# Hybrid attention, state-space and rwkv blocks on one core: decay-row loads issued from GpSimd's queue

## The chip, the cores and the metric

One core of a Trainium2 chip runs the whole program. The metric is the device time of one execution in microseconds (us), as the median of a few runs. The engines are named as in the profile: PE is the matrix engine (PEld its weight loads), DVE the vector engine, ACT the scalar engine, POOL is GpSimd, SP is the engine that here does nothing but issue DMAs. A trailing q (SPq, POOLq) marks an engine's sequencer. Each engine works through its own instructions strictly in order.

## The reference, cut to what matters

The program is a chain of blocks on 512 tokens of width 1024 (attention, a state-space scan, feed-forward layers, an rwkv scan, a second scan with matrix memory). The change lies in the state-space scan of the first block. Its decay matrix is built per chunk of 128 tokens and per head from the cumulated log decay `la`:

```python
SSD_CHUNK = 128
def step(state, inp):                       # one chunk; 4 chunks, 32 heads in 4 groups of 8
    x_, dt_, b_, c_ = inp
    la = jnp.cumsum(dt_ * a, axis=1)
    seg = la[:, :, None] - la[:, None, :]
    decay = jnp.exp(jnp.where(causal, seg, -jnp.inf))
    cb = jnp.einsum('bign,bjgn->bijg', c_, b_)
    xdt = x_ * dt_[..., None]
    y_intra = jnp.einsum('bijg,bijgh,bjghp->bighp', cb, decay, xdt)
    y_inter = jnp.einsum('bign,bghpn->bighp', c_, state) * jnp.exp(la)[..., None]
    to_end = jnp.exp(la[:, -1:] - la)
    new_state = (state * jnp.exp(la[:, -1])[..., None, None]
                 + jnp.einsum('bjgn,bjgh,bjghp->bghpn', b_, to_end, xdt))
    return new_state, y_intra + y_inter
```

## The kernel before, in words

All matmuls that matter are done in three passes of split weights: `wload` (L294 to L305) brings a 512 KB block of weights into `wraw` from SP's queue, ACT rounds it to `whi` (L302), DVE computes the rest `wlo` (L303), and PE multiplies `wlo`, `whi` and `whi` again (L311 to L313, or L394 to L396). `wraw`, `whi` and `wlo` have three buffers each, so a weight load waits for the readers of the block three before it.

In the state-space stage four groups of heads are worked through one behind another, and three strands are merged in turn: `group(g)` (the scan of group g, `ssd_core`, then its output product `ssd_out`), `ssd_in(g + 1)` (input products, convolution and transposes of the next group) and pieces of `ada_units`, a product that belongs to a later block and only fills PE's time: it loads two blocks of `ada_w` into `wraw` (L1039), multiplies them straight from there (L1042, into `pso`) and adds the result to `adr` on DVE (L1045, L1047). The fourth group's scan is merged with the gate products (`w_gate`, L849 to L851) and the rest of the `ada` pieces, and has no input products beside it.

Inside `ssd_core`, each of the 4 chunks takes 8 heads in two halves. For a half, L778 loads 4 rows of 128 cumulated log decays from `lad`, a small DRAM tensor, to all 128 partitions (tile `La`, 128 x 4 x 128, 256 KB written, rows of 512 bytes). DVE subtracts the column value and clips at zero, one head at a time (L781, four instructions), ACT takes the exponential in place (L782), DVE multiplies by the masked product of C and B (`cbm`) into `MT` (L784). PE then multiplies `MT` with `xdt` (L789). The state is carried by L804 (PE), L809 and L810 (DVE), and enters the next chunk by L796 (PE). There are 4 x 4 x 2 = 32 such loads. `La` has three buffers, so a load waits until L784 has read the half three before.

The convolution is `conv_silu` (L703 to L714): ACT evicts the product to `cacc` (L709), DVE adds three shifted terms (L711), ACT takes tanh (L713), DVE closes it into `xst`, `BT` or `CT` (L714).

The order of instructions on each engine is not that of the source: a scheduler simulates the program and sets each engine's order from when it thinks operands are there. Where a DMA is issued is therefore part of what sets the order on the other engines. At run time every engine follows the fixed order and waits on semaphores.

In this stage GpSimd has nothing to do: its last work before it are small DMAs of the attention's last step (L613, L629, L633), the next one is an addition in the last output product (L944).

Of the kernel before, what the change touches and what calls it, by code (L numbers as in the profile page):

```python
# [18 lines left out]
P = 128  # L19
# [240 lines left out]
class Kern:  # L260
# [494 lines left out]
    def ssd_core(self, pool, g, inp):  # L755

        nc, D = self.nc, self.D
# [8 lines left out]
        for c in range(4):  # L766
            ct = slice(c * P, (c + 1) * P)
            ps = self.btile()[:, :P]
            nc.tensor.matmul(ps, BT[:, ct], CT[:, ct], start=True, stop=True)
            cbm = pool.tile([P, P], F32, name="cbm")  # L770
            V_.tensor_tensor(cbm, ps, self.triu, op=ALU.mult)
            xdt = pool.tile([P, 512], F32, name="xdt")
            V_.tensor_tensor(hv(xdt), hv(xs[:, c]), bc(self.dtt[:, c, h8]), op=ALU.mult)
            MTs = []
            for half in range(2):
                E = pool.tile([P, 4, P], F32, name="La", bufs=3)
                hs = slice(8 * g + 4 * half, 8 * g + 4 * half + 4)
                nc.sync.dma_start(E, self.lad[hs, ct].unsqueeze(0).to_broadcast([P, 4, P]))  # L778
                for k in range(4):
                    h = 8 * g + 4 * half + k  # L780
                    V_.tensor_scalar(E[:, k], E[:, k], self.lat[:, c, h:h + 1], 0.0, op0=ALU.subtract, op1=ALU.min)  # L781
                S_.activation(E, E, AF.Exp)  # L782
                MT = pool.tile([P, 4, P], F32, name="MT", bufs=3)
                V_.tensor_tensor(MT, E, cbm.unsqueeze(1).to_broadcast([P, 4, P]), op=ALU.mult)  # L784
                MTs.append(MT)
                yield
            yi = self.psO.tile([P, 512], F32, name="pso")
            for k in range(8):
                nc.tensor.matmul(yi[:, k * 64:(k + 1) * 64], MTs[k // 4][:, k % 4], xdt[:, k * 64:(k + 1) * 64],  # L789
                                 start=True, stop=True)  # L790
            y = pool.tile([P, 512], F32, name="tmp", bufs=4)
            V_.tensor_tensor(hv(y), hv(xs[:, c]), bc(self.dsk[:, h8]), op=ALU.mult)
            V_.tensor_tensor(y, yi, y, op=ALU.add)
            if c > 0:
                yx = self.btile()
                nc.tensor.matmul(yx, CT[:, ct], state, start=True, stop=True)  # L796
                t = pool.tile([P, 512], F32, name="tmp", bufs=4)
                V_.tensor_tensor(hv(t), hv(yx), bc(self.ela[:, c, h8]), op=ALU.mult)
                V_.tensor_tensor(y, y, t, op=ALU.add)
            if c < 3:  # L800
                xw = pool.tile([P, 512], F32, name="tmp", bufs=4)
                V_.tensor_tensor(hv(xw), hv(xs[:, c]), bc(self.wend[:, c, h8]), op=ALU.mult)
                ps = self.btile()
                nc.tensor.matmul(ps, Bt[:, c], xw, start=True, stop=True)  # L804
                new = pool.tile([P, 512], F32, name="state")
                if state is None:
                    S_.copy(new, ps)
                else:
                    V_.tensor_tensor(hv(new), hv(state), bc(self.etot[:, c, h8]), op=ALU.mult)  # L809
                    V_.tensor_tensor(new, ps, new, op=ALU.add)  # L810
                state = new
                yield
            V_.scalar_tensor_tensor(yg[:, c], y, 0.5, zs[:, c], op0=ALU.mult, op1=ALU.mult)
            S_.activation(y, yg[:, c], AF.Square, accum_out=ss[:, c:c + 1])
# [1519 lines left out]
```

## Time and profile before

| | us |
|---|---|
| median of 3 runs | 3330.66 (3327.07 to 3337.02) |
| the profiled execution | 3335.31 |
| its span, first to last instruction | 3333.5 |
| PE busy in the span | 3125.6 (94%) |
| DVE, ACT, POOL busy | 1977.9, 1392.0, 225.0 |

The state-space scan runs from about 390 us to 830 us of the span. In a timeline a row gives start, duration, engine, line, operation, output and inputs, shape and count; in square brackets stands how long the engine was idle just before, and whose end released it. An x2 or x16 behind a row means that so many instructions of one kind ran behind one another. A wait is put down to the one event that came last.

### The profile page before, as it was taken

The numbers are of one execution on the slowest core, as the hardware profiler recorded it, in microseconds if no ns is written. First come the engines' busy times: TensorE is split into PE (matmuls) and PEld (weight loads), VectorE is DVE, ScalarE is ACT, GpSimd is POOL, SyncE is SP. The second block draws the span as 40 slices with busy tenths as digits, with TensorE's granted clock in tenths as the row PEclk, the third lists the DMA queues.
The fourth block names the chain that finished last, engine by engine and source line by source line (L and its number), as shares of the span: only waits on it lengthen the run. The fifth ranks groups of instructions, "written<-read, shape, count | busy, mean of one in ns | idle before, by whom it ended". The sixth has DMA issues, their size and how long they took to land.

```text
span 3333.5 us, 57556 instructions
## 1 busy us (share of the span) xinstructions
PE 3125.6 (94%) x23870; PEld 2490.3 (75%) x23870; DVE 1977.9 (59%) x3286; ACT 1392.0 (42%) x2387; POOL 225.0 (7%) x325
## 2 busy tenths in 40 slices
PE   8999999999999999899798999989999899999998
PEld 7777777776777788666477788678788667778887
DVE  4344576775655533557665566567385754775756
ACT  3344334333354432435444455355432454543323
POOL 0000000000100000022111111000000210000001
PEclk9999999999999999899799999989999999999999
DMA  6222344345534432434555554622222425222233
GB/s 203 87 65 71 123 151 148 117 133 193 166 119 128 129 112 95 149 102 148 164 171 185 178 181 141 238 93 94 102 95 95 139 86 188 82 104 97 95 99 108
DMA packets 216518, 431.00 MB, mean 129 GB/s; under 512 B 75114, under 2 KB 114218, under 8 KB 216000
## 3 DMA queue, kind: packets, MB, share of 16 engines
q1 hardware_dynamic: 192896, 367.59, 34.2%
q10 hardware_dynamic: 20912, 51.64, 4.2%
q0 software_dynamic: 2448, 8.09, 0.8%
q8 instruction: 187, 3.06, 0.4%
q14 instruction: 75, 0.61, 0.1%
HBM read 380.46 MB, written 46.79 MB: 128 GB/s over the span
## 4 chain that ended last, share of the span: by engine, by line
PE 75%; DVE 10%; DMA 7%; ACT 4%; issue 3%; POOL 1%; SPq 0%; ACTq 0%; POOLq 0%; DVEq 0%
PE psa L311 12%; PE psa L313 12%; PE psa L312 12%; PE psa L394 6%; PE psa L395 6%; PE psa L396 6%; PE pso L311 3%; DVE wlo L303 2%; PE pso L312 2%; PE pso L313 2%; ACT whi L302 1%; PE pso L1042 1%; DMA wraw<-in_f_up_dram 1%; PE psa L1601 1%; PE pso L789 1%
## 5 line engine op out<-in xcount | busy, mean ns | idle before, releaser
L303 DVE TENSOR_TENSOR wlo<-wraw,whi 128x1024 fp32r<-128x1024 f32 x480 | 593.5, 1238 | 497.8 <-ACT whi L302 494.9
L302 ACT CAST whi<-wraw 128x1024 fp32r<-128x1024 f32 x482 | 503.6, 1047 | 757.2 <-PE psa L396 255.9
L311 PE MATMUL psa<-xh,wlo 128*128 128x512 f32 (+1 forms) x1760 | 696.0, 397 | 12.9 <-DVE wlo L303 8.9
L313 PE MATMUL psa<-xh,whi 128*128 128x512 f32 (+1 forms) x1760 | 687.2, 391 | 0.0
L312 PE MATMUL psa<-xl,whi 128*128 128x512 f32 (+1 forms) x1760 | 685.1, 390 | 0.0
L311 PEld LDWEIGHTS psa<-xh,wlo 128*128 128x128 f32 x1760 | 338.6, 193 | 89.2 <-DVE wlo L303 11.0
L313 PEld LDWEIGHTS psa<-xh,whi 128*128 128x128 f32 x1760 | 338.2, 192 | 73.5 <-issue 5.1
L312 PEld LDWEIGHTS psa<-xl,whi 128*128 128x128 f32 x1760 | 338.9, 193 | 70.4 <-issue 2.9
L1163 DVE SCALAR_TENSOR_TENSOR fc<-psa,f_cv,fc 128x441 f32<-128x441 f32 (+2 forms) x352 | 243.4, 692 | 40.8 <-ACT fc L1152 33.9
L311 PE MATMUL pso<-xh,wlo 128*128 128x256 f32 (+1 forms) x720 | 230.7, 320 | 3.0 <-DVE wlo L303 2.1
L312 PE MATMUL pso<-xl,whi 128*128 128x256 f32 (+1 forms) x720 | 221.0, 307 | 1.0 <-DVE xl L357 1.0
L313 PE MATMUL pso<-xh,whi 128*128 128x256 f32 (+1 forms) x720 | 220.7, 307 | 0.0
L395 PE MATMUL psa<-wlo,ah 128*128 128x512 f32 x528 | 211.6, 401 | 2.7 <-DVE wlo L303 2.4
L394 PE MATMUL psa<-whi,al 128*128 128x512 f32 x528 | 209.7, 400 | 3.4 <-ACT whi L302 3.4
L396 PE MATMUL psa<-whi,ah 128*128 128x512 f32 x528 | 210.4, 399 | 0.0
L311 PEld LDWEIGHTS pso<-xh,wlo 128*128 128x128 f32 x720 | 135.9, 189 | 16.6 <-issue 6.5
L312 PEld LDWEIGHTS pso<-xl,whi 128*128 128x128 f32 x720 | 136.1, 189 | 8.7 <-DVE xl L357 1.6
L313 PEld LDWEIGHTS pso<-xh,whi 128*128 128x128 f32 x720 | 135.9, 189 | 7.9 <-issue 1.2
L395 PEld LDWEIGHTS psa<-wlo,ah 128*128 128x128 f32 x528 | 99.4, 188 | 30.0 <-DVE wlo L303 6.2
L394 PEld LDWEIGHTS psa<-whi,al 128*128 128x128 f32 x528 | 99.3, 188 | 29.6 <-ACT whi L302 4.7
L394 PE MATMUL psa<-whi,xl 128*128 128x512 f32 x288 | 116.4, 406 | 2.9 <-DVE acc L940 1.5
L396 PEld LDWEIGHTS psa<-whi,ah 128*128 128x128 f32 x528 | 99.5, 188 | 23.5
(570 smaller groups left out, 4985.1 us busy)
## 6 DMA issues: line engine op xcount, KB each, us to landing
wraw<-in_f_up_dram SPq DMA_DIRECT2D x132, 512.0 KB
wraw<-in_ada_w_dram SPq DMA_DIRECT2D x96, 512.0 KB
wraw<-in_f_dn_dram SPq DMA_DIRECT2D x66, 512.0 KB
wraw<-in_w_fi_dram SPq DMA_DIRECT2D x44, 512.0 KB
wraw<-in_ab_f_dram SPq DMA_DIRECT2D x38, 512.0 KB
wraw<-in_w_qk_dram SPq DMA_DIRECT2D x24, 512.0 KB
wraw<-in_w_xbc_dram SPq DMA_DIRECT2D x24, 512.0 KB
wraw<-in_c_f_dram SPq DMA_DIRECT2D x24, 512.0 KB
```

The source lines that it names most:

```text
L302: nc.scalar.copy(hi, raw)
L303: (eng or nc.vector).tensor_tensor(lo, raw, hi.bitcast(F32), op=ALU.subtract)
L311: mm(ps, wl, xh, start=start, stop=False)
L312: mm(ps, wh, xl, start=False, stop=False)
L313: mm(ps, wh, xh, start=False, stop=stop)
L394: mm(ps, sl, wh[:, c], start=first and k == 0, stop=False)
L395: mm(ps, sh, wl[:, c], start=False, stop=False)
L396: mm(ps, sh, wh[:, c], start=False, stop=last and k == kbn - 1)
L789: nc.tensor.matmul(yi[:, k * 64:(k + 1) * 64], MTs[k // 4][:, k % 4], xdt[:, k * 64:(k + 1) * 64], start=True, stop=True)
L1042: nc.tensor.matmul(ps[o:o + 32], self.cs[:, 4 * h + j, 22 - 2 * i:54 - 2 * i], raw[:, j * 256:(j + 1) * 256], start=h == 0, stop=h == 1, t ...
L1163: V_.scalar_tensor_tensor(o, pv[:, r0 + dr:r1 + dr, c0 + dc:c1 + dc], cw(i), o, op0=ALU.mult, op1=ALU.add)
L1601: mm(ps[h, d, b], lt[h, d, b], rt[h, d, b], start=True, stop=True, tile_position=(32 * q, 32 * q))
```

## The change

The 32 loads of L778 are issued from GpSimd's queue instead of SP's. Nothing else is written differently.

```diff
             for half in range(2):
                 E = pool.tile([P, 4, P], F32, name="La", bufs=3)
                 hs = slice(8 * g + 4 * half, 8 * g + 4 * half + 4)
-                nc.sync.dma_start(E, self.lad[hs, ct].unsqueeze(0).to_broadcast([P, 4, P]))
+                nc.gpsimd.dma_start(E, self.lad[hs, ct].unsqueeze(0).to_broadcast([P, 4, P]))
                 for k in range(4):
                     h = 8 * g + 4 * half + k
```

On SP's queue the loads leave, and the weight loads keep their order among themselves. On GpSimd's queue all 32 stand one behind another with nothing between them. The scheduler, which now sees the loads on a free queue, also sets DVE, ACT and PE in another order at some places of the stage. Numbers behind a name tell the buffers of one tile apart.

DVE at the start of the stage (`La_3155` is the first of all loads, `cacc_2832` a convolution of the first group's inputs):

```order
 L685 COPY dtla_2849<-psb_2840 128x256
 L714 SCALAR_TENSOR_TENSOR CT_2668<-ctan_2779,cacc_2774 128x512
+L781 TENSOR_SCALAR La_3155<-La_3155,dtla_2849 128x128
 L711 SCALAR_TENSOR_TENSOR cacc_2832<-psa_2800,conv1_2657,cacc_2832 128x511
 L781 TENSOR_SCALAR La_3155<-La_3155,dtla_2849 128x128
```

The first subtraction of the first load moves ahead of a convolution step that stood before it.

DVE in the first group, around the load of chunk 2, second half (`La_3582`; groups two and three have the same piece):

```order
 L784 TENSOR_TENSOR MT_3433<-La_3426,cbm_3359 128x512
 L714 SCALAR_TENSOR_TENSOR xst2_3332<-ctan_3338,cacc_3333 128x512
+L781 TENSOR_SCALAR La_3582<-La_3582,dtla_2849 128x128 x2
 L711 SCALAR_TENSOR_TENSOR cacc_3404<-psa_3372,conv1_2657,cacc_3404 128x511
 L1047 TENSOR_TENSOR adr_2645<-pso_3412,adr_2645 128x256
```

Two of its four subtractions move ahead of a convolution step and of the addition to `adr`.

DVE in the fourth group, around the load of chunk 2, second half (`La_6047`); `state_5966` is the state that L796 reads next, `wlo_5901` a block of gate weights:

```order
 L1047 TENSOR_TENSOR adr_2645<-pso_5875,adr_2645 128x256
+L781 TENSOR_SCALAR La_6047<-La_6047,dtla_2849 128x128
 L810 TENSOR_TENSOR state_5966<-psb_5964,state_5966 128x512
 L771 TENSOR_TENSOR cbm_6020<-psb_6018,masks_89 128x128
-L809 TENSOR_TENSOR state_6124<-state_5966,ela_2893 128x512
+L781 TENSOR_SCALAR La_6047<-La_6047,dtla_2849 128x128
 L303 TENSOR_TENSOR wlo_5901<-wraw_5899,whi_5900 128x1024
 L784 TENSOR_TENSOR MT_6031<-La_6024,cbm_6020 128x512
+L781 TENSOR_SCALAR La_6047<-La_6047,dtla_2849 128x128 x2
 L798 TENSOR_TENSOR tmp_6117<-psb_6115,ela_2893 128x512
-L781 TENSOR_SCALAR La_6047<-La_6047,dtla_2849 128x128 x4
```

The first subtraction of this load now stands ahead of the step that completes the state, L810; in the order before all four stood far behind it.

## Rows read from the trace of the kernel before

**Rows 1.** Stretches: length, busy of PE, PEld, DVE, ACT, POOL, clock, DMA, GB/s.

```profile
750.00:800.00 50.00, 44.25 (x263) 29.73 (x263) 29.24 (x63) 11.63 (x19) 0.00 (x0) 0.97 0.66 224
sum 440.00, PE 424.15 PEld 325.02 DVE 308.85 ACT 170.99 POOL 0.00; mean PE 47.13 PEld 36.11 DVE 34.32 ACT 19.00 POOL 0.00
```

**Rows 2.** Waits, PE, 387 to 826 us: total us, times, longest.

```profile
PE pso L1042 <- DMA wraw<-in_ada_w_dram: 6.6, 4, 3.0
PE pso L1042 <- DVE cacc L711: 5.0, 2, 2.6
PE psb L743 <- DVE xst L714: 1.2, 1, 1.2
PE psb L796 <- DVE state L810: 1.1, 2, 0.6
```

**Rows 3.** Waits, SP's queue, 360 to 830 us.

```profile
SPq L301 <- DVE wlo L303: 152.9, 34, 18.9
SPq L1039 <- PE pso L1042: 78.0, 19, 8.6
SPq L778 <- DVE MT L784: 30.6, 22, 4.2
```

**Rows 4.** Tile La: instructions (ns min/median/max), and who waits for its load.

```profile
L778 SPq DMA_DIRECT2D La<-lad x32: 377/377/750, 392.9 to 774.7; - x32
...
  DMA La<-lad: 15.3, 5
```

**Rows 5.** Timeline of all engines, 461 to 469 us, group one.

```profile
461.15 1.28 DVE L784 TENSOR_TENSOR MT<-La,cbm 128x512 f32<-128x512 f32 x2
461.86 0.98 SPq L778 DMA_DIRECT2D La<-lad  x2
465.30 0.82 SPq L1039 DMA_DIRECT2D wraw<-in_ada_w_dram  x2
465.52 0.75 DVE L711 SCALAR_TENSOR_TENSOR cacc<-psa,conv,cacc 128x511 f32<-128x511 f32 x1 [2.48 <-ACT cacc L709]
467.17 1.21 DVE L303 TENSOR_TENSOR wlo<-wraw,whi 128x1024 fp32r<-128x1024 f32 x1
468.71 0.59 PE L1042 MATMUL pso<-wraw,cs 128*32 128x256 f32 x2 [1.99 <-DMA wraw<-in_ada_w_dram]
```

**Rows 6.** DMAs that GpSimd issues: tiles B (512 KB, 512-byte rows), Wb, R; landings.

```profile
L468 POOL DMA_DIRECT2D B<-scr x2: 889/892/894, 39.6 to 50.1; - x2
DMA to landing us min/median/max: 4.4/6.4/9.8
L633 POOL DMA_DIRECT2D Wb<-dw x8: 597/611/620, 197.1 to 338.3; - x8
DMA to landing us min/median/max: 3.6/4.7/6.1
L613 POOL DMA_DIRECT2D R<-dstat x4: 564/585/774, 186.3 to 324.6; - x4
```

**Rows 7.** Timeline, SP and DVE, 388 to 442 us.

```profile
392.89 1.49 SPq L778 DMA_DIRECT2D La<-lad  x3
397.84 0.29 DVE L781 TENSOR_SCALAR La<-La,dtla 128x128 f32<-128x128 f32 x1 [1.66 <-DMA La<-lad]
438.04 0.98 SPq L778 DMA_DIRECT2D La<-lad  x2
441.80 1.66 DVE L781 TENSOR_SCALAR La<-La,dtla 128x128 f32<-128x128 f32 x8 [3.19 <-DMA La<-lad]
```

**Rows 8.** Timeline of all engines, 766 to 772 us, group four.

```profile
766.63 1.29 DVE L784 TENSOR_TENSOR MT<-La,cbm 128x512 f32<-128x512 f32 x2
770.29 0.39 SPq L778 DMA_DIRECT2D La<-lad  x1
770.90 0.69 DVE L810 TENSOR_TENSOR state<-psb,state 128x512 f32<-128x512 f32 x1 [0.60 <-PE psb L804]
771.65 1.12 PE L796 MATMUL psb<-state,CT 128*128 128x512 f32 x2 [0.56 <-DVE state L810]
```

## The prediction

> **What bounds the kernel now.** I read the stretches first. From 390 to 830 us, the stage with the loads, PE is busy 424.15 of 440 us; 15.9 us are idle, 5.75 of them between 750 and 800 [rows 1]. The reader is to see that PE is the bound here and that GpSimd does nothing at all (0.00). So the change can win at most the part of 15.9 us that hangs on the moved loads or on what stands behind them in SP's queue, and it can lose wherever a later `La` holds up something that PE waits for.
>
> Second, what ends PE's waits [rows 2]. `L1042 <- ada_w` (6.6 us) and `L1042 <- cacc L711` (5.0 us) are one pattern. In group one PE stands 1.99 us at 468.71 for an `ada_w` block that was issued 3.4 us earlier, at 465.30 [rows 5]. I read the two waits put down to L711 likewise, since L1042 reads the same kind of block there and L711 writes nothing that it reads. No wait of PE names `La`. Two name what may stand behind it: `L743 <- xst` (1.2 us) and `L796 <- state` (1.1 us).
>
> Third, SP's queue and the loads themselves. SP waits 30.6 us at L778 for MT, 22 times, but its weight loads wait 152.9 us for `wlo` and 78.0 us for L1042 [rows 3]: weights wait for their own buffers. DVE waits for a load 5 times, 15.3 us in all [rows 4]; at 441.80 it is 3.19 us [rows 7], and PE shows no wait there.
>
> **What leaves SP.** 32 issues of 377 ns at the median [rows 4] are 12 us of SP's time, and 30.6 us of its waiting go too. Of this nothing is on the path as far as the rows tell: behind the two loads of 461.86, which end at 462.84, the next weight load leaves only at 465.30 [rows 5], because its buffer is still being read. After the load of 770.29 the same holds. I take 0. The cover is the three `wraw` buffers; were it gone, the block would come earlier by at most the 0.98 us of an issue pair. Below zero the bound is the `ada_w` waits themselves, 6.6 + 5.0 us: it would need the blocks to arrive before PE asks, though SP may issue them only after PE released the buffer.
>
> **What a load costs on GpSimd.** No `La` load from there is in the trace. The nearest row is `B`, the same 512-byte rows but twice as many: 0.89 us to issue, and the fastest of that tile landed after 4.4 us. `Wb`, the same 256 KB in longer rows, takes 0.6 us to issue and lands after 3.6 to 6.1 us, 4.7 at the median [rows 6]. From SP the pair of 438.04 was there at 441.80, 3.8 us after the issue, and the first load of 392.89 at 397.84, 4.95 us, behind other weights [rows 7]. So a load from GpSimd takes 3.6 to 5.2 us (the upper end is the landing of 512 KB, 4.4, plus an issue of 0.8), against 3.8 to 4.95. I take 4.4, the row with the same 512-byte rows, and keep both ends; the 6.1 of the slowest `Wb` is left to the second rival. On a queue of its own it no longer stands behind the weights, and the weights no longer stand behind it. The 32 issues, some 0.75 us each by the two rows (24 us), hide in GpSimd's 440 idle us [rows 1]; in its queue each waits for L784 as before, and what queues behind is only the next such load.
>
> **What the new order costs.** These are the places where a wait for a load is put ahead of something that PE needs.
>
> 1. Start. The load issued at 392.89 lands at 396.5 to 398.1. DVE then has one L711 (0.66 us from start to start) and one L781 (0.2 us, 1.66 for eight [rows 7]) more before the chain to `xst`, for which PE stands 1.2 us [rows 2]. Against 397.84 the chain moves by -1.34 + 0.86 = -0.5 to +0.3 + 0.86 = +1.1 us; with 4.4 us by 397.3 - 397.84 + 0.86 = +0.3.
>
> 2. Groups one to three, chunk 2. `La_3582` is issued at 461.86, as the first of its pair, and lands at 465.5 to 467.1. The two subtractions (0.4 us) end at 465.9 to 467.5, and L711, which began at 465.52, starts 0.4 to 2.0 us later. Behind it is `wlo`, done at 468.38, which PE asks for at 469.3, after its L1042 of 468.71 [rows 5]: slack 0.9 us. Cost 0 to 1.1 us, by 4.4 us 0.2; I take the same slack for all three groups: 0 to 3.3, taken 0.5.
>
> 3. Group four. `La_6047` may now leave when the first L784 of 766.63 ends, about 767.3, where SP sent it at 770.29 because other waits stood before it [rows 8]. It lands at 770.9 to 772.5, plus 0.2 us for the subtraction that now stands before L810. L810 began at 770.90, and PE already stood idle for it (0.56 us) [rows 8], so there is no slack: 0.2 to 1.8 us, by 4.4 us 1.0.
>
> 4. Crowding. This load and the one behind it now move bytes some 3 us earlier, while gate and `ada_w` blocks are on their way. A 256 KB share of a stage that moved 224 GB/s [rows 1] is about 1.2 us of its bandwidth; 0 to 1.2 us, taken 0.2, since the PE waits named are already counted.
>
> Sum: 0.3 + 0.5 + 1.0 + 0.2 = +2.0 us; the ends are -0.5 and 1.1 + 3.3 + 1.8 + 1.2 = +7.4 us. After the stage no engine's order differs. The profiled execution took 3335.3 us, so the sum against it is 3337.3; it stood 4.65 us above the median of the three runs, so for a median I forecast 3330.66 + 2.0 = 3332.7 us. A difference of 0.3%, 10 us, is about what a measurement of this kernel can tell from no change; the three runs themselves differ by 9.95 us.
>
> **A rule against this change.** The Trainium skill (SBUF — State Buffer, "SBUF: two separate sides") says that descriptors of a DMA issued from GpSimd are written by GpSimd's cores, and that these are locked out while DVE runs an operation in a mode that takes both of its ports, an fp32 copy within SBUF for example; a DMA issued from SP or ACT is immune. The trace neither confirms nor excludes it: eight `Wb` issues took 597 to 620 ns, one of four `R` issues 774 instead of 564 [rows 6]. What it would make of the time is the second rival.
>
> **Rivals.**
>
> *SP is set free and weights come earlier.* For it: 42 us of SP's time leave. If every `ada_w` block came before PE asks, the 6.6 + 5.0 us would go [rows 2]: 3332.7 - 11.6 = 3321 us. Against it: the block of 465.30 left 2.5 us after the last load's issue had ended [rows 5]. Chance 0.05. The Trainium skill (DMA: Bandwidth & Descriptors, "Issuing engines are not separate DMA queues") says that spreading issues over engines saves only the issuing time; by that rule this rival is out.
>
> *Loads land late (slower).* GpSimd's descriptors are held up by DVE, which is busy 308.85 of 440 us [rows 1]. Every load then lands later by x than taken above. Eight places would feel it: the start, three in groups one to three, group four, and the three pairs like that of 441.80, where DVE stands still for a load. With x = 2.5 us (two `wlo` of 1.2 us in the way), the start and group four pay 2.5 each, and the three places of point 2 pay 2.5 less the 0.7 of slack left, 1.8 each; the pairs, whose slack no row shows, 0 to 2.5 each, say 1.25. That is 5.0 + 5.4 + 3.8 = 14 us on top of the 2.0: 3347 us. It passes 0.3% from x of about 1.6 us on. Against it: issues of 0.6 us for `Wb` in a stage where DVE works as well. Chance 0.10.
>
> *The queues share the DMA engines worse.* `La` bytes now run beside the `ada_w` block that PE waits for, instead of ahead of it. If each of the 6 waits for `ada_w` [rows 2] grew by 0.6 us (half of the 1.2 us above): +3.6, 3336 us, still no difference that can be told. Chance 0.10.
>
> *The change does nothing* that the clock shows, because the loads leave at the same moment from either queue and the order costs nothing: 3330.7 us. Chance 0.25.
>
> **How the numbers follow.** The forecast, 3332.7 us, has the remaining 0.50. The sum's ends, -0.5 and +7.4, and the spread of the runs, 3327 to 3337, make up the range: 3330.7 - 0.5 - 4 = 3326 to 3332.7 + 7.4 + 2 = 3342, where I leave out most of the first rival (3321) and of the second (3347). Faster by over 0.3% means below 3320.7: most of the first rival, 0.04. Slower by over 0.3% means above 3340.7: the second rival and a tail of the forecast, 0.09. The rest, 0.87, is within 0.3%.
>
> **What would show it.** In the changed kernel's profile SP has no L778 row and the weight loads leave at the same moments after their `wraw` readers; a load takes about 4.4 us from GpSimd's issue to DVE's first L781; L1042 still waits some 2 us for `ada_w` in each group; DVE waits for `La` about as often as before, and a new wait stands ahead of L711 near 463 us and of L810 near 770 us, with PE's wait at L796 longer by about 1 us. PE's idle time in the stage is 16 to 20 us. It is wrong if that idle time falls below 10 us (SP did matter), if loads take 6 us or more (descriptors are held up), or if time moves behind 830 us, where nothing was changed.

## The result, and the profile after

The changed kernel takes 3351.31 us (median of five runs, 3345.47 to 3355.45) against 3330.66 us: a ratio of 1.0056, 95% interval 1.0038 to 1.0074. Forecast were 3332.7 us and a range up to 3342. It is slower by 0.56%, and a second set of runs below gives 1.0049.

The profiled execution took 3355.45 us, its span is 3353.3 us. I take as the stage what lies between the first load's issue and the last L824 (the transposes that close group four). Before it ran from 392.9 to 831.7 us, 438.8 us; now from 395.1 to 857.5 us, 462.4 us, 23.6 us longer. Ahead of it 2.2 us were lost, and behind it 6.0 us gained, both in code and order that did not change; two profiles of the kernel before differ by 9 us there (e18, below), so this says nothing.

PE's waits from 387 to 850 us (total, times, longest), the answer to [rows 2]:

```profile
PE pso L1042 <- DMA wraw<-in_ada_w_dram: 14.4, 4, 4.6
PE pso L1042 <- DVE cacc L711: 4.6, 1, 4.6
PE psb L796 <- DVE state L810: 4.4, 2, 3.8
PE psb L743 <- DVE xst L714: 2.1, 1, 2.1
```

L1042 waits 19.0 us where it waited 11.6, L796 4.4 where it waited 1.1, L743 2.1 where it waited 1.2: 11.6 us more. The stretches say the same, and more. Columns are length, busy time of PE, PEld, DVE, ACT and POOL, the granted clock, the DMA share and GB/s. Of after, the piece behind the wait at L743, the pieces that begin in or behind the five longest waits, and the stage:

```profile
416.30:419.70 3.40, 3.40 (x11) 2.71 (x10) 2.75 (x4) 1.37 (x2) 0.00 (x0) 0.50 0.09 24
...
474.30:481.10 6.80, 4.74 (x11) 3.19 (x12) 6.42 (x13) 2.84 (x4) 0.00 (x0) 0.50 0.38 130
583.50:590.30 6.80, 5.74 (x13) 4.03 (x14) 5.86 (x13) 2.84 (x4) 0.00 (x0) 0.50 0.30 99
692.80:699.60 6.80, 5.73 (x13) 3.98 (x14) 5.30 (x12) 2.84 (x4) 0.00 (x0) 0.50 0.27 93
791.80:798.50 6.70, 5.02 (x17) 2.51 (x18) 5.39 (x14) 1.12 (x2) 0.75 (x1) 0.50 0.44 126
819.10:825.80 6.70, 5.39 (x20) 3.90 (x21) 1.23 (x1) 1.64 (x2) 0.00 (x0) 0.50 0.46 166
390.00:860.00 470.00, 442.39 (x2289) 336.26 (x2289) 314.27 (x573) 172.81 (x257) 23.84 (x32) 0.96 0.43 139
```

Of the kernel before, the 6.8 us behind its wait in group one, the two pieces at half clock that it has, and the stage:

```profile
468.70:475.50 6.80, 6.79 (x37) 4.95 (x40) 5.54 (x14) 2.90 (x5) 0.00 (x0) 1.00 0.34 111
676.40:679.80 3.40, 3.12 (x7) 1.95 (x8) 3.40 (x10) 0.69 (x2) 0.00 (x0) 0.50 0.53 174
795.90:799.30 3.40, 3.40 (x14) 2.69 (x11) 0.50 (x1) 0.00 (x0) 0.00 (x0) 0.51 0.62 201
390.00:834.00 444.00, 428.02 (x2278) 327.61 (x2277) 312.85 (x571) 172.33 (x255) 0.00 (x0) 0.99 0.45 147
```

PE's idle time rose from 16.0 (444.00 - 428.02) to 27.6 us (470.00 - 442.39), by the 11.6 us of the waits. And the granted clock, 1.00 behind the wait of 1.99 us, is 0.50 (1.2 instead of 2.4 GHz) behind each of the longer ones. PE is busy 26.6 us in the five rows at 0.50, and 3.4 in the first. At full clock this work takes about half (matmuls of 128x512 start every 0.43 us behind the wait in group one, every 0.23 us ahead of it), so by this estimate 15.0 us are lost. In the kernel before the two pieces hold 6.5 us of work, 3.3 us lost. The difference, 11.7 us, and the 11.6 us of waiting are 23.3 of the 23.6 us. **In this profile half of the stage's loss is waiting, half is the clock behind the waits.**

The loads themselves: tile La (ns min/median/max, first and last start; then landing in us; then DVE's waits for the load, total and times), against [rows 4]:

```profile
L778 POOL DMA_DIRECT2D La<-lad x32: 747/747/771, 395.1 to 796.1; - x32
...
  DMA La<-lad: 40.4, 12
...
DMA to landing us min/median/max: 3.7/4.4/6.6
```

And group one, to be read against [rows 5] (start, duration, engine, line, operation; in brackets the idle time before and its releaser):

```profile
466.30 1.28 DVE L784 TENSOR_TENSOR MT<-La,cbm 128x512 f32<-128x512 f32 x2
467.51 1.48 POOL L778 DMA_DIRECT2D La<-lad  x2 [21.97 <-ACT ctan L713]
470.44 0.80 SPq L1039 DMA_DIRECT2D wraw<-in_ada_w_dram  x2
472.09 0.48 DVE L781 TENSOR_SCALAR La<-La,dtla 128x128 f32<-128x128 f32 x2 [3.91 <-DMA La<-lad]
474.14 1.21 DVE L303 TENSOR_TENSOR wlo<-wraw,whi 128x1024 fp32r<-128x1024 f32 x1
476.37 1.03 PE L1042 MATMUL pso<-wraw,cs 128*32 128x256 f32 x2 [4.50 <-DMA wraw<-in_ada_w_dram]
```

The pair of loads leaves 2.93 us ahead of the `ada_w` blocks, about as before (3.44 us). The block is issued when PE frees its buffer, as before, but PE has it 5.93 us later instead of 3.41 us. The same stands in groups two and three (waits of 4.6 us against 2.4 and 2.6). In group four it is another chain:

```profile
785.88 0.68 DVE L784 TENSOR_TENSOR MT<-La,cbm 128x512 f32<-128x512 f32 x1
786.49 1.49 POOL L778 DMA_DIRECT2D La<-lad  x2 [15.44 <-DVE MT L784]
788.29 1.13 PE L804 MATMUL psb<-tmp,Bt 128*128 128x512 f32 x2
792.54 0.29 DVE L781 TENSOR_SCALAR La<-La,dtla 128x128 f32<-128x128 f32 x1 [3.69 <-DMA La<-lad]
792.74 0.68 DVE L810 TENSOR_TENSOR state<-psb,state 128x512 f32<-128x512 f32 x1
793.48 1.22 PE L796 MATMUL psb<-state,CT 128*128 128x512 f32 x1 [3.84 <-DVE state L810]
```

The first load of the pair takes 6.0 us, one subtraction that now stands ahead of L810 waits for it, and PE waits 3.84 us for the state instead of 0.56 [rows 8].

### The profile page after: what moved, and what is told of

It reads as the page before. It is cut to its first block, busy times and chain, and to the rows that moved or that the text cites. A ratio compares the mean times of both kernels' runs of the same rounds, so it can differ in the third digit from the quotient of the medians.

```text
span 3353.3 us, 57577 instructions
## 1 busy us (share of the span) xinstructions
PE 3135.6 (94%) x23870; PEld 2493.4 (74%) x23870; DVE 1976.9 (59%) x3286; ACT 1391.1 (41%) x2387; POOL 245.2 (7%) x357
## 4 chain that ended last, share of the span: by engine, by line
PE 76%; DVE 10%; DMA 6%; ACT 4%; issue 3%; POOL 1%; SPq 0%; ACTq 0%; POOLq 0%; DVEq 0%
PE psa L311 12%; PE psa L313 12%; PE psa L312 11%; PE psa L395 6%; PE psa L394 6%; PE psa L396 6%; PE pso L311 3%; PE pso L312 3%; PE pso L313 3%; DVE wlo L303 2%; PE pso L1042 1%; PE psa L1601 1%; ACT whi L302 1%; PE pso L789 1%; DMA wraw<-in_f_up_dram 1%
## 5 line engine op out<-in xcount | busy, mean ns | idle before, releaser
L311 PEld LDWEIGHTS pso<-xh,wlo 128*128 128x128 f32 x720 | 137.2, 191 | 17.1 <-issue 6.9
```

Source lines behind the costliest of these rows:

```text
L311: mm(ps, wl, xh, start=start, stop=False)
```

## The experiments

My theory was that the loads' way does the harm: GpSimd sends them later and their bytes hold the `ada_w` block up. The rival was that the scheduler's new order does it, since the change moves rows on PE, DVE, ACT and SP too. To part the two, a kernel is built twice in one program: the first pass only yields an order, the second pass is bound to it by edges that set the order of issue and make nothing wait. Only the place of the loads is left to the scheduler. Code below is cut, and set against the kernel before.

```diff
-                nc.sync.dma_start(E, self.lad[hs, ct].unsqueeze(0).to_broadcast([P, 4, P]))
+                getattr(nc, LOADS).dma_start(E, self.lad[hs, ct].unsqueeze(0).to_broadcast([P, 4, P]))
...
+                if prev is not None:
+                    tc.add_manual_dep(i, prev, mybir.DependencyInfo(mybir.DependencyClass.NoSync,
+                                      mybir.DependencyReason.DATA), reason="order")
...
+    order = program(arrays, "sync")[1]
+    nc = program(arrays, "gpsimd", order)[0]
```

Each set of runs has its own runs of the kernel before (medians 3329.9 to 3333.0 us); ratios are to those, and a ratio need not be that of the two medians.

| kernel | loads from | order of | us | ratio, 95% interval | stage us | PE idle us | at half clock, us |
|---|---|---|---|---|---|---|---|
| before | SP | before | 3330.66 | | 438.8 | 16.0 | 6.8 |
| e18, before again | SP | before | 3332.04 | 1.0006 (0.9996 to 1.0017) | 441.1 | 16.6 | 10.2 |
| after | GpSimd | after | 3351.31 | 1.0056 (1.0038 to 1.0074) | 462.4 | 27.6 | 37.5 |
| e9, after again | GpSimd | after | 3350.41 | 1.0049 (1.0031 to 1.0066) | 461.2 | 27.2 | 30.7 |
| e1 | GpSimd | before | 3343.01 | 1.0029 (1.0020 to 1.0038) | 455.2 | 25.7 | 23.9 |
| e2 | SP | after | 3343.37 | 1.0032 (1.0020 to 1.0045) | 457.6 | 23.9 | 30.7 |
| e3 | ACT | before | 3333.31 | 0.9992 (0.9977 to 1.0008) | 445.5 | 17.0 | 17.1 |
| e10, half the bytes | GpSimd | before | 3332.34 | 1.0002 (0.9989 to 1.0016) | 443.2 | 16.8 | 13.7 |
| e13, two issues | GpSimd | before | 3359.02 | 1.0085 (1.0060 to 1.0111) | 466.4 | 32.0 | 30.7 |
| e14, 2 KB rows | GpSimd | before | 3345.10 | 1.0039 (1.0022 to 1.0056) | 455.6 | 25.5 | 23.9 |

The last three columns come from one profile each; two profiles of one kernel differ by about 2 us in the stage (before and e18, after and e9), and by 3.4 and 6.8 us in the time at half clock. The profile of e2 is of an execution of 3354.49 us, 11 us above e2's median, so its row shows e2 at its worst. For the halves named above, e9 against e18 says the same as after against before: 10.6 us more idle time and 20.5 us more at half clock, in a stage 20.1 us longer.

### Queue or order (e1, e2, e9)

Expected of e1:

> The 32 La loads are issued by GpSimd, as in the changed kernel, but every engine's other instructions stand in the order of the kernel before: the queue without the new order. Theory A (the loads' way: they start later after their buffer is free and their bytes travel beside the ada_w block that PE waits for): slow like the changed kernel, 3345 to 3353 us, PE's waits for ada_w in groups one to three about 4.5 us each. Theory B (the scheduler's new order of DVE, PE and ACT did it): like the kernel before, 3328 to 3336 us, waits for ada_w of about 2 us.

Expected of e2 (the same edges; first pass "gpsimd", second "sync"):

> The loads are issued by SyncE, as before, but PE, DVE, ACT and GpSimd stand in the order of the changed kernel: the order without the queue. Theory A: like the kernel before, 3327 to 3338 us. Theory B: like the changed kernel, 3345 to 3355 us, with PE's waits for ada_w of about 4.5 us in groups one to three and the wait at L796 of about 3.8 us in group four.

Expected of e9:

> The changed kernel itself, to stand beside e1 and e2 on one more set of runs. If queue and order each cost what e1 and e2 measured (+9.6 and +10.7 us) and the costs add, 3333 + 20 = 3353 us, 3348 to 3356. If they overlap (both lengthen the same waits), 3343 to 3347.

Neither theory alone holds. The queue costs 10.1 us (3343.01 - 3332.95) and the order 10.4 us; their sum, 20.5, stands beside 18.7 (e9) and 20.7 us (after), as far as intervals of some 3 to 6 us to either side can tell. PE's waits of e1 and then of e2 show that they are two different losses:

```profile
PE pso L1042 <- DMA wraw<-in_ada_w_dram: 20.2, 6, 4.8
PE psb L796 <- DVE state L810: 1.1, 2, 0.6
```

```profile
PE pso L1042 <- DMA wraw<-in_ada_w_dram: 10.4, 4, 3.3
PE psb L796 <- DVE state L810: 6.0, 2, 5.5
PE pso L1042 <- DVE cacc L711: 2.6, 1, 2.6
PE psb L743 <- DVE xst L714: 2.1, 1, 2.1
```

The queue alone lengthens the waits for `ada_w` (20.2 us where before had 6.6 + 5.0) and leaves L796 alone. The order alone leaves those nearly as they were and makes PE stand 5.5 us for the state.

### What it is about GpSimd's queue (e3, e10, e13, e14)

Expected of e3 (second pass "scalar"):

> The loads are issued by ScalarE, in a queue of their own as on GpSimd, all else in the order of the kernel before. It tells a queue of its own from GpSimd as the issuer. If it is the queue of its own that lets La's bytes crowd the ada_w block: ada_w waits of 4 us or more and 3345 us or above. If it is GpSimd's later start (0.5 us after the buffer is free, against 0.03 us on SyncE) and its slower bytes: ada_w waits of about 2 us, 3328 to 3340 us, the upper end for ScalarE's own waiting at these issues.

A queue of its own is not the trouble: from ACT's queue the loads cost nothing that can be told. This also shows that freeing SP is worth nothing that can be told here. In e3, the pair in group one, the block and PE's wait:

```profile
463.08 0.97 ACTq L778 DMA_DIRECT2D La<-lad  x2
466.51 0.81 SPq L1039 DMA_DIRECT2D wraw<-in_ada_w_dram  x2
470.44 1.03 PE L1042 MATMUL pso<-wraw,cs 128*32 128x256 f32 x2 [2.50 <-DMA wraw<-in_ada_w_dram]
```

The same three rows in e1:

```profile
462.80 1.49 POOL L778 DMA_DIRECT2D La<-lad  x2 [21.97 <-ACT ctan L713]
465.72 0.81 SPq L1039 DMA_DIRECT2D wraw<-in_ada_w_dram  x2
471.62 0.95 PE L1042 MATMUL pso<-wraw,cs 128*32 128x256 f32 x2 [4.47 <-DMA wraw<-in_ada_w_dram]
```

What the DMA engines moved, from 0.9 to 4.1 us after the block's issue, when its bytes flow (last two columns: share of the engines' time, GB/s), in the kernel before, in e3, in e1 and in e10 (half the bytes, below):

```profile
466.20:469.40 3.20, 1.21 (x5) 0.30 (x4) 3.20 (x6) 0.22 (x1) 0.00 (x0) 1.00 0.96 330
```

```profile
467.40:470.60 3.20, 0.70 (x3) 0.18 (x2) 3.20 (x6) 0.48 (x2) 0.00 (x0) 0.93 0.96 316
```

```profile
466.60:469.80 3.20, 0.55 (x2) 0.00 (x0) 3.20 (x6) 0.25 (x1) 0.00 (x0) 1.00 0.92 282
```

```profile
464.90:468.10 3.20, 0.94 (x4) 0.14 (x2) 3.20 (x6) 0.22 (x1) 0.00 (x0) 1.00 0.95 325
```

With loads from GpSimd the engines are almost as busy but move 282 instead of 330 GB/s. By the packets' records of the two traces, La's bytes flow for 2.6 us in the kernel before and are in 0.9 us after the block's issue, when the block's first piece starts (at 1.0); in e1 they flow for 3.1 us, and until 1.7, beside the block. GpSimd also starts the pair 0.5 us later (1.22 against 0.71 us after the start of the L784 pair that frees the buffers). The last piece of the two blocks then starts 5.0 us after the issue, against 4.0. That is 1 us; PE gets its block 2.5 us later.

The rest lies in the parts of the block that land last. For each block the trace records 16 updates of the semaphore that PE waits for, and PE starts 0.13 to 0.14 us behind the last of them. In groups one to three of the kernel before the middle ones come 3.1 us after the issue and the last at 3.3, 3.7 and 4.0. In e1 the middle ones come at 3.4, 3.9 and 3.4, which is 0.3 to 0.8 us later, but the last at 5.8, 6.0 and 6.1. In e3 the last come at 3.7 to 3.9. So the slower flow is the small part of the delay, and the large one is in the last few updates. Which of the 16 DMA engines ran behind, the trace does not tell.

Nor does any load that still flows beside the block do this. In group three of the kernel before La's bytes flow until 2.2 us after the block's issue, in e3 until 2.1, longer than in e1 (1.9), and the last updates come at 4.0 and 3.9 us against 6.1. With the overlap alike, the issuer makes the difference.

Expected of e10:

> e1_queue_only with loads of half the size: two rows instead of four, 128 KB, and the subtractions of the other two read the first two (the decay factors of half the heads are therefore other numbers). If La's bytes in GpSimd's queue are what holds the ada_w block back, half of the extra wait goes: PE's waits for ada_w in groups one to three 3.0 to 3.5 us instead of 4.5 to 4.8, time 3336 to 3340. If it is a fixed cost of a load from GpSimd, the waits stay at 4.3 us or more and the time at 3341 to 3345.

```diff
-                nc.sync.dma_start(E, self.lad[hs, ct].unsqueeze(0).to_broadcast([P, 4, P]))
+                rows = FLAGS.get("rows", 4); getattr(nc, LOADS).dma_start(E[:, :rows], self.lad[hs, ct][:rows].unsqueeze(0).to_broadcast([P, rows, P]))
...
-                    V_.tensor_scalar(E[:, k], E[:, k], self.lat[:, c, h:h + 1], 0.0, op0=ALU.subtract, op1=ALU.min)
+                    V_.tensor_scalar(E[:, k], E[:, k % rows], self.lat[:, c, h:h + 1], 0.0, op0=ALU.subtract, op1=ALU.min)
```

Neither expectation came true. With half the bytes not half but all of the extra wait is gone: 2.26, 2.40 and 2.52 us in groups one to three, the flow at 325 GB/s, the time that of the kernel before. An issue still takes 710 ns (747 in full), so the issue is not the price.

Expected of e13:

> e1_queue_only with each load as two issues of two rows, 128 KB each: the same bytes, the same 512-byte rows, twice the issues. If the bytes in GpSimd's queue hold ada_w back, or a limit on rows in flight, as e1: waits for ada_w of 4.3 to 5 us and 3341 to 3347 us. If it is the size of one issue (e10's half-size loads were free), waits of about 2.5 us and 3330 to 3336 us.

```diff
+    q.dma_start(E[:, :2], rows[:2].unsqueeze(0).to_broadcast([P, 2, P]))
+    ADDED.append(q.dma_start(E[:, 2:], rows[2:].unsqueeze(0).to_broadcast([P, 2, P])).ins.name)
```

The same bytes in two issues are no remedy: waits of 4.5 to 5.0 us again, and new ones at L804 (6.5 us in three). The time, 3359.02 us, is 12 us above the longest that was expected. DVE now waits for La 20 times instead of 8, and L802, for which L804 waits, stands behind such subtractions.

Expected of e14:

> e1_queue_only with lad stored by chunks, so that a load is one 2 KB row for each partition instead of four rows of 512 bytes: the same bytes, a quarter of the pieces. If the number of pieces is what costs on GpSimd's way, the loads land 0.5 us or more earlier, the waits for ada_w fall to 2 to 3 us and the time to 3330 to 3337 us. If the bytes cost, as e1: 3340 to 3346 us.

```diff
-        self.lad = self.dram.tile([32, SEQ], F32, name="lad")
-        nc.scalar.dma_start(self.lad, la)
+        self.lad = self.dram.tile([4, 32, P], F32, name="lad")
+        nc.scalar.dma_start(self.lad.rearrange("c h p -> h c p"), la.rearrange("h (c p) -> h c p", c=4))
...
-                nc.sync.dma_start(E, self.lad[hs, ct].unsqueeze(0).to_broadcast([P, 4, P]))
+                getattr(nc, LOADS).dma_start(E.rearrange("p a b -> p (a b)"), self.lad[c, hs].rearrange("h p -> (h p)").unsqueeze(0).to_broadcast([P, 512]))
```

A quarter of the rows makes the issue shorter (538 ns) but not the landing (4.3 us) nor the waits in groups one to three (4.6 to 5.3 us). So what counts is the amount of bytes that GpSimd's queue has under way beside the block, and neither the number of issues nor the rows as they are written. The size of the pieces that the DMA engines move stays a rival that no run tests: in the packets' records the 32 loads from GpSimd are 2048 packets of 4096 bytes in e1 and in e14 alike, while the same loads are 16384 packets of 512 bytes from SP and ACT. e17 put the same 2 KB rows on SP's queue, where they are 4096 packets of 2048 bytes. Expected:

> The kernel before with lad stored by chunks, so that a load on SyncE is one 2 KB row for each partition instead of four of 512 bytes; all engines in the same order. PE waits for no La there, so if only what PE waits for counts: 3327 to 3335 us, no difference that can be told. If shorter DMA time ahead of the ada_w blocks helps them: their waits fall from 2.0 to 2.6 us to 1.5 or less and the time to 3320 to 3326 us.

It gave 3332.45 us, ratio 0.9999 (0.9987 to 1.0010): no gain, waits of 2.2 to 2.5 us in groups one to three.

### Is it paid at L1042 alone (e5, e6, e11, e12, e4)

Expected of e5:

> Loads on GpSimd in the order of the kernel before (as in e1_queue_only), and L1042 reads a tile that is there already instead of the ada_w block; the block is still loaded into its wraw buffer, so bytes and queues stay, and only PE's waiting for it goes (the ada sums are therefore other numbers). Theory A (the price of GpSimd's queue is paid at L1042 alone, and in the clock behind it): the same as e6_other_operand_sp within 5 us, 3318 to 3325 us. Rival (the loads from GpSimd cost elsewhere as well, at DVE or in later weights): 8 to 12 us longer than e6.

Expected of e6:

> The control of e5: loads on SyncE, order of the kernel before, L1042 reads a tile that is there already instead of its ada_w block. PE's 11.6 us of waiting at L1042 should go and with them the two short stretches at half clock (6.8 us, worth 3.4): 3333 - 15 = 3318 us, 3316 to 3324.

```diff
-                                     raw[:, j * 256:(j + 1) * 256], start=h == 0, stop=h == 1, tile_position=(0, o))
+                                     read(self, raw, l, j), start=h == 0, stop=h == 1, tile_position=(0, o))
...
+    if l == 0 and FLAGS.get("other"):
+        return K.cs.rearrange("p a b -> p (a b)")[:, 58 * j:58 * j + 256]
```

e5 takes 3328.14 us (0.9993, 0.9978 to 1.0009), e6 3330.33 us (0.9999, 0.9987 to 1.0012). With no reader of the block the loads from GpSimd cost nothing that the whole time tells. But the pair of runs is weaker than I had meant it to be, for two reasons. The edit takes away more than PE's wait: SP, which waited 78.0 us at L1039 for L1042 in the kernel before, no longer waits for it at all, so the blocks leave at other moments; in group one of e5 they leave at 452.1 and 455.8 us, and the pair of loads only at 462.6, so the two do not meet there (nor in groups two and three). And in the profiles e5's stage is 436.6 us, 6.2 us longer than e6's, with 6.8 us at half clock against none. What shows better that most of the queue's price is paid at L1042 is e1 itself: of its 9.7 us more of idle time (25.7 against 16.0) 8.6 are at L1042 (20.2 against 11.6 us). That it is paid there alone is not shown.

But my size for e6 was wrong: in its profile the stage is 430.4 us, 8 to 11 us shorter, with no time at half clock, and yet the whole is at most 4 us shorter. Where the rest goes, I could not find: the stretch behind the stage took 2499 us, between what the two profiles of the kernel before show there (2502 and 2492).

Expected of e11:

> Loads on SyncE; only the last of the five ada units in each of groups one to three, the one that PE waits for, yields between its two blocks, so other work stands between them. e6 took all waiting for ada_w away and came out 2 us shorter than the kernel before; so 3327 to 3333 us, with PE's waits at L1042 in groups one to three below 1 us and the stage 4 to 7 us shorter in the profile. If the new order makes another wait, 3333 to 3340.

Expected of e12:

> e11 with its order kept and the loads on GpSimd. Theory A (GpSimd's queue costs through the ada_w wait of L1042): where that wait has slack the queue costs little, e11 plus 0 to 4 us (the wait in group four stays). Rival (it costs wherever the load goes late): e11 plus 8 to 11 us, as e1 against the kernel before.

```diff
-                        merge(group(g), self.ssd_in(sp, g + 1, xT, inp), islice(ada, 5))
+                        merge(group(g), self.ssd_in(sp, g + 1, xT, inp), islice(ada, 6))
...
-                self.work += 0.9
+                h and l == 0 and g in (4, 9, 14) and (yield); self.work += 0.9
```

This did not take the wait away: L1042 still stands 2.5 us in each group (12.3 us for `ada_w` in all), since the first of the two blocks is the one that is late. e11 takes 3338.56 us (1.0017, 1.0006 to 1.0029). So e12, 3350.06 us (1.0049, 1.0035 to 1.0064), could not show slack; it shows the queue's price once more, 11.5 us over e11, with waits of 3.7 to 4.5 us. An earlier form with every unit split, e4, has this expectation:

> Loads on SyncE as before; an ada_w unit of two blocks (2 x 512 KB, back to back) yields between its blocks, so that other work stands between them on PE and no two of them are asked for at once. If PE's waits for ada_w (6.6 + 5.0 us in the kernel before) come from two blocks in a row with three wraw buffers, PE's idle time in the stage falls from 15.9 to 6 to 10 us and the time to 3317 to 3325 us. If the scheduler or the buffers only move the wait, 3328 to 3335 us.

```diff
+                if l == 0 and h == 0:
+                    yield
...
-                        merge(group(g), self.ssd_in(sp, g + 1, xT, inp), islice(ada, 5))
+                        merge(group(g), self.ssd_in(sp, g + 1, xT, inp), islice(ada, 10))
```

It cut PE's idle time in the stage to 9.3 us, as expected, but the time is 3339.16 us, 1.0010 (0.9998 to 1.0023), no gain. In its profile the last of the `ada` matmuls came behind the scan of group four (until 833.1 us, the last L824 at 828.3); that this is where the gain went is not shown.

### What it is about the order (e7, e15, e16)

Expected of e7 (orders of both passes; the edges of after ahead of group four, those of before from there on):

> e2_order_only (loads on SyncE, order of the changed kernel) with group four and all behind it back in the order of the kernel before. If the order's price is the one wait at L796 for state in group four (5.46 us against 0.56) and the half clock behind it (6.8 us, worth 3.4), the time is that of the kernel before plus 1 to 2 us: 3331 to 3337. If the order costs in groups one to three too (the wait at L743, ada_w waits of 2.5 to 3.2 us that drop the clock), 3338 to 3343.

Expected of e15 (edges of after for DVE only):

> Loads on SyncE; VectorE alone in the order of the changed kernel (subtractions ahead of L711 and of L810), PE, ACT, GpSimd and SyncE as before. If VectorE's order makes what e2 measured: 3338 to 3345 us, the wait at L743 about 2 us and that at L796 in group four 3 us or more. If it is PE's order: 3330 to 3335 us.

Expected of e16 (edges of after for PE only):

> Loads on SyncE; PE alone in the order of the changed kernel, all else as before. If VectorE's order makes the cost of e2: 3330 to 3335 us. If it is PE's order: 3338 to 3345 us.

```diff
+    order = {e: (after if e == "EngineType.DVE" else before)[e] for e in before}
+    nc = program(arrays, "sync", order)[0]
```

e7 takes 3339.57 us (1.0019, 1.0006 to 1.0032), e15 3339.33 us (1.0028, 1.0011 to 1.0045), e16 3337.93 us (1.0027, 1.0009 to 1.0045). DVE's order holds the one clear mechanism. In e15, group four:

```profile
773.97 0.39 SPq L778 DMA_DIRECT2D La<-lad  x1
779.22 0.29 DVE L781 TENSOR_SCALAR La<-La,dtla 128x128 f32<-128x128 f32 x1 [5.24 <-DMA La<-lad]
779.42 0.69 DVE L810 TENSOR_TENSOR state<-psb,state 128x512 f32<-128x512 f32 x1
780.16 1.22 PE L796 MATMUL psb<-state,CT 128*128 128x512 f32 x1 [5.39 <-DVE state L810]
```

```profile
779.30:789.50 10.20, 9.34 (x30) 6.16 (x31) 4.75 (x12) 1.68 (x2) 0.00 (x0) 0.50 0.57 153
```

The subtraction for the late load stands ahead of L810, PE stands 5.39 us, and the next 10.2 us run at half clock (the last row is a stretch, in the columns above). With group four's order undone (e7) some 4 us come back against e2, which is within the two intervals. What remains, 6 to 7 us, lies in groups one to three, and no single wait is seen to hold it: in e7's profile, of an execution 10 us below e7's median, L743 waits 2.9 us (1.2 before, but 2.6 in e17, which has the order of before), and each of the waits for `ada_w` of 2.4 to 2.6 us has 3.4 us at half clock behind it. That PE's order alone costs 8 us (with an interval from 3 to 15) I had not expected, and its profile does not show where: stage 444.9 us, PE idle 19.4. This part stays open. DVE's and PE's share do not add up: 9.4 and 8.0 us alone, 10.4 together (e2).

### The clock (e8)

Expected:

> e1_queue_only with 18 matmuls of 128x512 (some 3.8 us), whose result is overwritten, put ahead of L1042 at the four units where PE stands 4.2 to 4.8 us for ada_w. Nothing that PE waits for comes earlier. If the half clock behind these stalls (17 us more of it in the stage than before, worth 8.5) comes from PE's standing still, the stage's half-clock time falls below 10 us and the time from 3343 to 3334 to 3338. If the clock has another cause, 3341 to 3346.

```diff
+    if l == 0 and (g, h) in FLAGS.get("fill", ()):
+        for _ in range(FLAGS["count"]):
+            ADDED.append(K.nc.tensor.matmul(full, K.xT0[:, 0, :P], K.xT0[:, 1], start=True, stop=True).ins.name)
```

Two rows of it in group one:

```profile
468.77 4.69 PE L2325 MATMUL pso<-xh 128*128 128x512 f32 x18
474.32 0.62 PE L1042 MATMUL pso<-wraw,cs 128*32 128x256 f32 x2 [0.86 <-DMA wraw<-in_ada_w_dram]
```

Its stage as a stretch (the seventh figure is the granted clock):

```profile
393.00:842.00 449.00, 441.15 (x2343) 338.39 (x2342) 310.63 (x569) 172.20 (x255) 23.88 (x32) 1.00 0.45 145
```

With PE at work while the block is late (the 5.9 us from issue to use are now 6.4), the clock stays at full throughout the stage: 0 us at half clock instead of 23.9, and the stage is 445.6 us instead of 455.2 although 72 matmuls were added. So it is PE's standing still that lowers the clock there; the section "HAM oscillation — how this bites in real kernels" of the Trainium skill's page "TensorE: Matmul & The Clock Gate" tells of such a kernel, in which waits for DMAs cost the clock as well, and this trace agrees. But the whole execution did not become shorter: 3345.20 us (1.0042, 1.0025 to 1.0058) against e1's 3343.01. In its profile the stretch behind the stage is 2505.0 us, with 172 us at half clock, against 2495.3 us with 155 in e1. Whether that is chance, as between the two profiles of the kernel before, or a loss that comes back later, five runs don't tell. Shown is what the clock does in the stage, not that its 9 us are to be had.

Expected of e18, the control (the kernel before, unchanged):

> The kernel before, unchanged: the ratio to itself within 0.2%, and a second profile of its stage. If the stage's length from the first load to the last L824 is a property of the kernel, 437 to 443 us with 5 to 15 us at half clock; if it strays by more than 8 us, the single profiles of e15 and e16 don't carry their readings.

The kernel before against itself gave 1.0006 (0.9996 to 1.0017), and the stage 441.1 against 438.8 us. So readings of the stage hold to some 3 us, those of the whole to some 5.

## Why the prediction was wrong

The direction was right, the size was off by a factor of nine to ten: +2.0 us forecast, +18.7 and +20.7 measured. Term by term:

- **What leaves SP: 0.** Right. From ACT's queue (e3) SP is just as free, and the time is that of before. The Trainium skill's rule that was set against the first rival (DMA: Bandwidth & Descriptors, "Issuing engines are not separate DMA queues"), that spreading issues over engines saves only the issuing time, agrees with e3 (0.9992). From GpSimd the same loads cost 9.7 us more than from ACT (e1 and e3, whose code differs in the issuer alone): the issuer has a price that the prediction did not hold.
- **The load's price: 4.4 us** taken, 4.4 measured at the median. Right. But the longest is 6.6 where I had capped it at 5.2, and the long ones are those that matter: 6.0 us in group four. The second rival (descriptors held up, every load later) fails: 32 issues of 747 to 771 ns, and the median as forecast.
- **Order, point 1 (start):** +0.3 taken, -0.5 to +1.1 the range; L743 waits 0.9 us more. Within the range, without the 3.4 us at half clock behind it.
- **Order, point 2 (groups one to three):** L711 does start late (472.49, after DVE stood 3.91 us for the load), but PE by then waits for `ada_w` anyway. Taken 0.5, visible 0.
- **Order, point 3 (group four):** the chain is the one described, L781 ahead of L810 ahead of L796. Taken 1.0 (0.2 to 1.8), measured 3.3, since the load landed after 6.0 us. In e15, with the loads on SP, the same wait is 4.8 us longer than before. The chain was right and the landing mis-sized.
- **Crowding, point 4: the step that failed.** Taken 0.2, at most 1.2, as one share of bandwidth. I had argued that the waits for `ada_w` were counted already; they were counted at their old length. They grew by 7.4 us (11.6 to 19.0). The third rival named exactly this, at 0.6 us for each of six waits; it was 2.0 to 2.5 us in each of groups one to three and 1.1 in group four. I took a block to be late by the competing bytes' time alone (256 KB at 224 GB/s); the runs show that loads of 256 KB from GpSimd slow the flow (282 against 330 GB/s, the middle of a block 0.3 to 0.8 us later) and, above all, that PE waits for the last pieces of the block, which come 2.1 to 2.5 us later (e1, groups one to three).
- **What no term held: the clock.** A longer wait was priced at its length. In the profile of the changed kernel each of the five longest also had 6.7 to 6.8 us at half clock around its end; with the 3.4 us behind L743's wait, and less what the kernel before had, that is 11.7 us lost, as much as the waits. This term was put at nothing without a reason, and with the crowding it makes most of the miss.
- **What no term held: the rest of the order.** I looked for places where a wait for a load is put ahead of something, and found the right ones; the scheduler also moved PE's rows, and e7 and e16 put a price of 6 to 8 us on order in which no such place is seen. What makes it stays open.

The prediction named as signs against it idle time below 10 us, loads of 6 us or more, and time behind 830 us. Of these only a load of 6.6 us came, and the length of the issues shows no descriptors held up. The signs that told were two that it had expected to hold: "L1042 still waits some 2 us for `ada_w` in each group" (4.5 to 4.6 us in groups one to three), and PE's idle time in the stage, 16 to 20 us (27.6).

## What to carry to other kernels

Before a load is given to another queue, look for the transfer that PE already waits for at that moment: its wait is not a fixed sum, and in this kernel bytes from GpSimd's queue lengthened it where the same bytes from SP or ACT did not. Price a PE wait of several us together with the clock in the rows right behind it. And where a scheduler places instructions by who issues what, a change of issuer is two changes; bind the order and measure each by itself.

## What was not expected of the hardware

- Loads of 256 KB from GpSimd raised the wait for another queue's block from 2.3 to 4.6 us, loads of 128 KB not at all (e10, 2.26 to 2.52 us). The cost is not in proportion to the bytes, and it lies in the last few of a block's 16 updates (in e1 13 of them are in by 3.9, 5.2 and 4.0 us, the last by 5.8 to 6.1). Why, these runs don't show.
- How much the clock adds to a wait: behind PE's wait of 1.99 us in group one it stayed at 2.4 GHz, at the one of 4.50 us at the same place 6.8 us, from within the wait on, ran at 1.2 GHz and held 4.74 us of work, 2.4 us lost. With other matmuls in the wait (e8) it stayed at 2.4 GHz. The length of a wait does not settle it alone: of the two profiles of the kernel before, both with a wait of 2.38 us in group two, one has 3.4 us at half clock behind it (e18) and one has none.
- A stage that is 8 to 10 us shorter in its profile (e6 against before, e8 against e1) did not make the execution shorter by as much, if at all.
